# Four pairs of column blocks per feed-forward stage from seven products, with couples of products summed in PSUM

## The chip, the cores and the metric

The kernel runs on one core of one Trainium2 chip. Its engines work beside one another and meet at semaphores: TensorE (PE, with its weight loads as PEld), VectorE (DVE), ScalarE (ACT), GpSimd (POOL) and SyncE (SP, here a queue of transfers). The metric is device time in microseconds, the median of several runs. A profile shows one execution.

## The reference

Two transformer blocks over one sequence of 256 positions with a model width of 1024, in fp32. Between them lie four feed-forward stages of one form, two in the first block and two in the second; the rest (convolution, attention, gated delta rule, shared keys and values) is not touched by the change.

```python
def swiglu_ffn(h, w13, w2):
    gate, up = jnp.split(h @ w13, 2, axis=-1)
    return (jax.nn.silu(gate) * up) @ w2
...
x = x + 0.5 * swiglu_ffn(rms_norm(x, ffn1_norm[l]), ffn1_w13[l], ffn1_w2[l])
```

`w13` is 1024 x 5632 (2816 gate columns, 2816 up columns) and `w2` is 2816 x 1024.

## The kernel before

**Precision.** A product of fp32 matrices is made of three matmuls (`mm3`): each operand is split into a high part and the rest, and high x high, rest x high and high x rest are summed in PSUM. A weight unit is 128 x 1024; ScalarE copies it into the high part `wh` (L442, every activation of the kernel is recorded at this line) and VectorE subtracts to get the rest `wl` (L445, likewise every two-operand operation of VectorE). There are seven `wh` and seven `wl` buffers, and a buffer comes free with the last matmul on it. Matmuls stand at L468 (at L746 in the changed kernel where they belong to a pair), transposes at L471.

**Blocks.** The hidden width is cut into eleven blocks *j* of 256 gate and 256 up columns, the sequence into two row tiles T of 128. A plain block takes 2 T x 8 k-tiles x 3 = 48 matmuls with 512 columns each (`single`, `singles`). `act` makes the hidden activations from a block's PSUM tile (a Silu on ScalarE, a scale-and-multiply on VectorE), `flip` transposes them (two PE transposes, a copy on ScalarE, a subtract on VectorE), and `outs(j)` multiplies them by `w2` (24 matmuls into the four `acc` tiles).

**Pairs.** Two blocks *j*, *j2* together are a 2 x 2 block product (row tiles by halves of the 1024 inputs by blocks), which the kernel makes of seven products in place of eight (`pair`), each of 12 matmuls: 84 in place of 96. The products take sums of the activations (`forms`, once per stage) and running sums of the weights, kept in the tiles `n["11"]`, `n["12"]`, `n["21"]`, `n["22"]` (two 128 x 1024 units each, pool `s4`). `raw` loads such a tile with transfers of SP's queue; `more` adds a second weight onto it by accumulating transfers that GpSimd issues (L726); `plus` adds on VectorE. Within p2 the tile "11" gets its second weight by `more`, so the sequence is: VectorE ends the split of "11" for p1, the accumulating transfer runs, and then the split for the next product on "11", p5, can start. Before, the order of products was p1, p2, p7, p5, p6, p3, p4, each in a PSUM tile of its own, and VectorE (ScalarE for p1 and p5) added each into the SBUF tiles `t[0]` to `t[3]`.

**Order.** Instructions of an engine run in the order in which a scheduler wrote them down; `merged` deals the steps of pairs among steps of `singles` and `outs` evenly, and `ahead` names a priority in a table of numbers that the change leaves as it is. The stages are f1, a mixer, f2 (about 323 to 500 us), the delta rule, f3, a small stage, the shared keys and values, f4, and the end. In each of f1 to f4 three pairs are made of products, (2,3), (5,6), (8,9), and the blocks 0, 1, 4, 7, 10 are plain.

Of the kernel before, what the change touches and what calls it, by code (L numbers as in the profile page):

```python
# [12 lines left out]
AF = mybir.ActivationFunctionType  # L13
ALU = mybir.AluOpType
# [7 lines left out]
NB = 11  # L22
# [339 lines left out]
class _Kernel:  # L362
# [254 lines left out]
    def ffn(self, gain, w13, w2, alpha, first=False):  # L617
        D = self.D
# [9 lines left out]
        def run(leave):  # L628
            acc = self.accs()
# [31 lines left out]
            def out(j, T):  # L661
                while any(p[:2] == (j, T) for p in pend):
                    flip()
                if j not in wu:
                    wu[j] = [self.unit(D[w2][2 * j + i], None, 4 + i) for i in range(2)]
                self.proj_out(acc[T], hid[j], (0, 1), T, wu[j], j == 0, j == NB - 1)


            def singles(j):
# [23 lines left out]
            def forms():  # L693

                F = self.t("b8", (8, 256))
                S = self.hilo("b8", (8, 256))
                q = [[(slice(None), slice(4 * k, 4 * k + 4), self.tsl(T)) for k in range(2)] for T in range(2)]
                with self.ahead("f.sum." + self.stage):
                    for T in range(2):
                        c = (slice(None), slice(None), self.tsl(T))  # L700
                        self.tt(F[c], h[0][c].bitcast(F32), h[1][c].bitcast(F32), ALU.add)
                    (f11, f12), (f21, f22) = [[F[c] for c in r] for r in q]
                    self.tt(f22, f22, f21, ALU.subtract)
                    self.tt(f21, f11, f21, ALU.subtract)
                    self.tt(f11, f22, f11, ALU.add)
                    self.tt(f12, f11, f12, ALU.subtract)
                    for T, k in ((1, 1), (0, 0), (1, 0), (0, 1)):
                        c = q[T][k]
                        self.split(S[0][c], S[1][c], F[c])
                return S  # L710

            def pair(j, j2, S):

                n, t = {}, []

                def raw(name, jj, k0):
# [17 lines left out]
                def prod(a_, T, k0, w):  # L734
# [6 lines left out]
                    ps = self.t("mm")  # L741
                    for k in range(4):
                        c = slice((k % 2) * 512, (k % 2) * 512 + 512)
                        self.mm3(ps, a_, (slice(None), k0 + k, self.tsl(T)), u[k // 2], (slice(None), c),
                                 k == 0, k == 3)
                    return ps  # L746

                def add(o, a_, ps, op=ALU.add):
                    with self.ahead("f.ev." + self.stage):
                        self.tt(t[o], t[a_], ps, op)  # L750

                def neg(o, a_, ps):
                    with self.ahead("f.ev." + self.stage):
                        self.stt(t[o], t[a_], -1.0, ps, ALU.mult, ALU.subtract)

                def p1():
                    tmp = self.t("b8", (4, 512))
                    t.extend(tmp[:, i] for i in range(4))
                    raw("11", j, 0)
                    raw("12", j2, 0)  # L760
                    more("12", j2, 2)
                    ps = prod(h, 0, 0, "11")
                    with self.ahead("f.ev." + self.stage):
                        self.act(t[0], ps, AF.Copy)

                def p2():
                    raw("21", j, 2)
                    more("11", j2, 0)
                    add(3, 0, prod(h, 0, 4, "21"))
                    act(j, 0, t[3])  # L770

                def p7():
                    raw("22", j2, 2)
                    add(1, 0, prod(S, 1, 0, "12"))

                def p5():
                    ps = prod(S, 1, 4, "11")
                    with self.ahead("f.ev." + self.stage):
                        self.act(t[2], ps, AF.Copy)

                def p6():
                    plus("11", "22")
                    ps = prod(S, 0, 0, "11")
                    add(1, 1, ps, ALU.subtract)
                    add(0, 0, ps, ALU.subtract)
                    add(0, 0, t[2])
                    neg(2, 1, t[2])
                    act(j2, 1, t[2])

                def p3():  # L790
                    neg(0, 0, prod(S, 0, 4, "22"))
                    act(j2, 0, t[0])

                def p4():
                    plus("11", "21")
                    add(1, 1, prod(h, 1, 4, "11"))
                    act(j, 1, t[1])

                return [p1, p2, p7, p5, p6, p3, p4]

            def merged(few, many):

# [16 lines left out]
                        flip()  # L819

            single(0)
            single(1)
# [9 lines left out]
            out(10, 0)  # L832
            leave(0, self.resid(acc[0], x[0], alpha))
            out(9, 1)
            out(10, 1)
            leave(1, self.resid(acc[1], x[1], alpha))

        return enter, run
# [865 lines left out]
```

## Time and profile before

| | |
|---|---|
| median of three runs | 1236.3 us (1235.31 to 1239.24) |
| profiled execution | 1234.6 us, its span 1232.6 us |
| PE | 1198.6 us busy, 97% of the span |
| VectorE | 1004.5 us busy, 81% |
| ScalarE | 741.3 us busy, 60% |
| GpSimd | 166.5 us busy, 14% |
| transfers | 234.38 MB, 190 GB/s in the mean |

Busy times are shares of the whole span. Spans of neighbouring matmuls overlap in the records, and so do neighbouring instructions of VectorE by some 0.08 us, so that the pace of a row of instructions is read from their starts.

### The profile page before, as it was taken

To read this page: it belongs to the slowest core of one execution; us is meant where nothing else is said; L and a number is where in the kernel's file an instruction comes from. 1 tells how busy PE (TensorE), PEld (TensorE's weight loads), DVE (VectorE), ACT (ScalarE), POOL (GpSimd) and SP (SyncE) were. 2 spreads that over 40 slices of the span, in tenths; PEclk is the share of its full clock that TensorE was granted. 3 is DMA by queue.
4 is the path that set the end of the run, shared out by engine and by line. 5 is a ranking of instruction groups with operands and counts; after the bars stand their busy time and mean duration, and the time that the engine had idled before them with its cause. 6 is when DMAs were issued, how large, how long until landed. Compare 5 with 4: busy or idle time off the path is not lost.

```text
span 1232.6 us, 17134 instructions
## 1 busy us (share of the span) xinstructions
PE 1198.6 (97%) x6248; PEld 1002.1 (81%) x6248; DVE 1004.5 (81%) x1482; ACT 741.3 (60%) x1134; POOL 166.5 (14%) x223
## 2 busy tenths in 40 slices
PE   8999999998999999998899999999999999999998
PEld 6788888986888888898898888888777788888887
DVE  6799987998788998689755888998776859889964
ACT  6566666346666665875313765666675747566653
POOL 1110002001101000226703101000121201010000
PEclk9999999999999999999999999999999999999999
DMA  8989463414679836355412689936445349698262
GB/s 284 303 275 295 115 208 127 159 38 154 222 239 292 283 91 217 127 203 162 137 52 69 242 252 285 279 102 210 161 151 175 111 144 302 257 295 217 92 199 80
DMA packets 72853, 234.38 MB, mean 190 GB/s; under 512 B 13496, under 2 KB 16224, under 8 KB 72640
## 3 DMA queue, kind: packets, MB, share of 16 engines
q1 hardware_dynamic: 61008, 204.14, 47.9%
q0 software_dynamic: 7168, 25.85, 11.0%
q10 hardware_dynamic: 4592, 3.29, 0.9%
q8 instruction: 49, 0.80, 0.3%
q14 instruction: 36, 0.29, 0.1%
HBM read 230.86 MB, written 2.37 MB: 189 GB/s over the span
## 4 chain that ended last, share of the span: by engine, by line
PE 79%; DVE 8%; DMA 4%; ACT 4%; issue 2%; POOL 1%; SPq 0%; DVEq 0%; ACTq 0%; POOLq 0%
PE mm L468 48%; PE acc L468 28%; DVE wl L445 3%; PE mm L471 3%; DMA wr<-w 2%; ACT s L442 1%; ACT wh L442 1%; DVE b L452 1%; DVE s L452 1%; DMA wr<-g_qkv 1%; POOL t L445 1%; DMA wr<-g_gate 1%; ACT b L442 1%; DMA s<-w 1%; ACT L442 1%
## 5 line engine op out<-in xcount | busy, mean ns | idle before, releaser
L468 PE MATMUL mm<-wh,b 128*128 128x512 f32 (+3 forms) x1808 | 571.5, 390 | 2.6 <-ACT wh L442 0.9
L445 DVE TENSOR_TENSOR wl<-wr,wh 128x1024 fp32r<-128x1024 f32 (+2 forms) x290 | 355.2, 1235 | 67.9 <-ACT wh L442 65.5
L442 ACT ACTIVATE wh<-wr 128x1024 fp32r<-128x1024 f32 (+2 forms) x290 | 303.8, 1056 | 157.6 <-PE mm L468 50.6
L468 PEld LDWEIGHTS mm<-wh,b 128*128 128x128 f32 x1808 | 333.4, 188 | 75.9 <-ACT b L442 1.9
L468 PE MATMUL mm<-wl,b 128*128 128x512 f32 (+3 forms) x904 | 349.2, 387 | 3.5 <-DVE wl L445 3.5
L468 PE MATMUL acc<-wh,s 128*128 128x512 f32 x768 | 254.9, 399 | 3.2 <-DVE s L452 3.1
L442 ACT ACTIVATE wh<-s 128x1024 fp32r<-128x1024 f32 x168 | 177.4, 1061 | 96.6 <-PE acc L468 33.0
L445 DVE TENSOR_TENSOR wl<-s,wh 128x1024 fp32r<-128x1024 f32 x168 | 202.8, 1220 | 30.2 <-ACT wh L442 29.7
L468 PEld LDWEIGHTS mm<-wl,b 128*128 128x128 f32 x904 | 170.0, 188 | 37.9 <-DVE wl L445 4.8
L468 PEld LDWEIGHTS acc<-wh,s 128*128 128x128 f32 x768 | 144.8, 189 | 36.9 <-ACT s L442 4.5
L468 PE MATMUL acc<-wl,s 128*128 128x512 f32 x384 | 153.4, 399 | 0.0
L468 PE MATMUL mm<-b,wh 128*128 128x256 f32 x640 | 118.3, 285 | 1.3 <-DVE b L452 1.3
L468 PEld LDWEIGHTS mm<-b,wh 128*128 128x128 f32 x640 | 98.7, 189 | 2.3 <-DVE b L452 1.5
L726 POOL DMA_DIRECT2D s<-w x48 | 41.9, 893 | 403.2 <-DMA s<-w 255.2
L468 PE MATMUL mm<-b,wl 128*128 128x256 f32 x320 | 89.3, 285 | 0.0
L468 PEld LDWEIGHTS acc<-wl,s 128*128 128x128 f32 x384 | 72.9, 190 | 16.2
L448 POOL TENSOR_SCALAR t<-t 128x1 f32<-128x1 f32 (+3 forms) x41 | 20.5, 499 | 462.5 <-ACT s L442 392.6
L452 DVE SCALAR_TENSOR_TENSOR b<-mm,cols,b 128x128 fp32r<-128x128 f32 (+4 forms) x164 | 62.3, 410 | 23.2 <-ACT b L442 22.7
L471 PE MATMUL mm<-const,s 128*128 128x128 f32 x336 | 66.4, 278 | 6.5 <-DVE s L445 3.0
L471 PEld LDWEIGHTS mm<-const,s 128*128 128x128 f32 x336 | 43.6, 142 | 21.3 <-DVE s L445 5.2
L468 PEld LDWEIGHTS mm<-b,wl 128*128 128x128 f32 x320 | 59.8, 189 | 0.2 <-DVE wl L445 0.2
L445 DVE TENSOR_TENSOR s<-s,s 128x1024 f32<-128x1024 f32 x48 | 57.7, 1218 | 0.3
(164 smaller groups left out, 1183.6 us busy)
## 6 DMA issues: line engine op xcount, KB each, us to landing
wr<-w SPq DMA_DIRECT2D x168, 512.0 KB, 4.9
s<-w SPq DMA_DIRECT2D x96, 512.0 KB, 6.9
s<-w POOLq DMA_DIRECT2D x48, 512.0 KB, 9.5
wr<-g_qkv SPq DMA_DIRECT2D x24, 512.0 KB, 4.3
wr<-pg SPq DMA_DIRECT2D x16, 512.0 KB, 4.2
wr<-w_kv SPq DMA_DIRECT2D x16, 512.0 KB, 4.0
wr<-w_ag SPq DMA_DIRECT2D x8, 512.0 KB, 4.3
wr<-w_qk SPq DMA_DIRECT2D x8, 512.0 KB, 4.7
```

Of the source, the lines that this page charges most:

```text
L442: return self.nc.scalar.activation(out=out, in_=in_, func=func, **kw)
L445: return (eng or self.nc.vector).tensor_tensor(out=out, in0=in0, in1=in1, op=op)
L448: return (eng or self.nc.vector).tensor_scalar(out=out, in0=in0, scalar1=s1, scalar2=s2, op0=op0, op1=op1)
L452: return self.nc.vector.scalar_tensor_tensor(out=out, in0=in0, scalar=scalar, in1=in1, op0=op0, op1=op1)
L468: return self.nc.tensor.matmul(out, lhsT=lhsT, rhs=rhs, start=start, stop=stop)
L471: return self.nc.tensor.transpose(out=out, in_=in_, identity=self.con("ident"))
L726: self.tc.keep_in_program_order(self.nc.gpsimd.dma_start(out=n[a_][i], in_=D[w13][jj][k0 + i], accum_op=ALU.add))
```

## The change

Each feed-forward stage makes four pairs of products, (2,3), (4,5), (6,7), (8,9), called the first to the fourth pair here, and keeps the blocks 0, 1 and 10 plain. The order within a pair is p1, p2, p5, p3, p6, p7, p4. Three couples share a PSUM tile: p2 is accumulated onto p1 (tile "A" of the code), p3 onto p5 ("D"), p7 onto p6 ("E"). Between the two products of a couple the first one's value is read out: ScalarE copies A into `t[0]` and D into `t[2]`, and VectorE subtracts `t[1]` from E. The accumulating transfers stay (two units onto "12", two onto "11" per pair), two `plus` add on VectorE as before, and with a fourth pair there are more of both. In f1 (`first`) the plain block 10 is dealt among the first pair's products; in the other stages block 1 is. The end of a stage has the outputs of blocks 8 and 9.

```diff
+                    ps = self.t("mm") if on is None else on
...
+                                stop=k == 3 and i == 2, skip_group_check=on is not None)
...
+                    n["A"] = prod(h, 0, 0, "11")
+                    ev(self.act, t[0], n["A"], AF.Copy)
 
                 def p2():
                     raw("21", j, 2)
                     more("11", j2, 0)
-                    add(3, 0, prod(h, 0, 4, "21"))
-                    act(j, 0, t[3])
+                    act(j, 0, prod(h, 0, 4, "21", n["A"]))
+
+                def p5():
+                    raw("22", j2, 2)
+                    n["D"] = prod(S, 1, 4, "11")
+                    ev(self.act, t[2], n["D"], AF.Copy)
+
+                def p3():
+                    plus("11", "22")
+                    ev(self.tt, t[1], t[0], prod(S, 0, 4, "22", n["D"]), ALU.add)
+
+                def p6():
+                    n["E"] = prod(S, 0, 0, "11")
+                    ev(self.tt, t[1], n["E"], t[1], ALU.subtract)
+                    act(j2, 0, t[1])
...
-                    raw("22", j2, 2)
-                    add(1, 0, prod(S, 1, 0, "12"))
...
-                    add(1, 1, ps, ALU.subtract)
-                    add(0, 0, ps, ALU.subtract)
-                    add(0, 0, t[2])
-                    neg(2, 1, t[2])
+                    plus("11", "21")
+                    ev(self.tt, t[0], t[0], prod(S, 1, 0, "12", n["E"]), ALU.subtract)
+                    ev(minus, 2, 0, t[2])
                     act(j2, 1, t[2])
...
-                return [p1, p2, p7, p5, p6, p3, p4]
+                return [p1, p2, p5, p3, p6, p7, p4]
...
-            few = pair(2, 3, S)
-            merged(few[:2], singles(4) + outs(0))
-            merged(few[2:], outs(1) + outs(4) + singles(7))
-            merged(pair(5, 6, S), outs(2) + outs(3) + outs(7))
-            merged(pair(8, 9, S), outs(5) + outs(6))
-            merged([], singles(10))
-            merged([], outs(8))
+            few, pB, pC, pD = (pair(j, j + 1, S) for j in (2, 4, 6, 8))
+            merged(few[:2], singles(10 if first else 1) + outs(0))
+            if first:
+                merged(few[2:] + pB + pC + pD, outs(1) + outs(10) + sum((outs(i) for i in range(2, 8)), []))
+            else:
+                merged(few[2:], outs(1) + singles(10))
+                merged(pB + pC + pD, outs(2) + outs(3) + outs(10) + sum((outs(i) for i in range(4, 8)), []))
```

The first place is ScalarE in f2, where the value of p1 is copied out. Before, in the last pair (8,9), the copy of p1's tile `mm_873` stands ahead of the two splits of "11" for p5 (`wh_898` and `wh_900`, from the tiles `s4_865` and `s4_866` which the accumulating transfers write):

```order
L442 ACTIVATE s2_861_4201<-mm_863_4203 128x2x128
L442 ACTIVATE wh_896_4329<-wr_895_4327 128x1024
L442 ACTIVATE b8_864_4208<-mm_873_4227 128x512
L442 ACTIVATE wh_898_4345<-s4_865_4209 128x1024
L442 ACTIVATE s2_861_4201<-mm_874_4241 128x2x128
L442 ACTIVATE s2_828_4055<-mm_875_4246 128x2x128
L442 ACTIVATE wh_900_4349<-s4_866_4210 128x1024
```

After the change, in the last pair of f2, also (8,9), the same copy (`b8_903` from `mm_912`) stands behind both splits of "11" for p5 (`wh_928`, `wh_930`):

```order
L442 ACTIVATE wh_924_4439<-wr_923_4437 128x1024
L442 ACTIVATE s1_885_4291<-b8_831_4058,t_638_3250 128x256
L442 ACTIVATE wh_928_4459<-s4_904_4365 128x1024
L442 ACTIVATE s1_895_4335<-b8_831_4058,t_638_3250 128x256
L442 ACTIVATE wh_930_4463<-s4_905_4366 128x1024
L442 ACTIVATE s2_900_4357<-mm_902_4359 128x2x128
L442 ACTIVATE wh_937_4490<-wr_936_4488 128x1024
L442 ACTIVATE b8_903_4364<-mm_912_4383 128x512
```

The copy moved from ahead of the two splits that need the transfer to behind them, and the next row shows that PE now needs it.

The second place is PE at the same point, from the last use of p1's second unit (`wl_911`) to the start of p2. Before, p2 starts a new tile, `mm_885`:

```order
L468 MATMUL mm_873_4227<-wl_872_4224,b8_600_3064 128x512
L468 MATMUL mm_873_4227<-wh_871_4223,b8_601_3065 128x512
...
L471 MATMUL mm_875_4246<-const_98,s1_860_4198 128x128 x2
L468 MATMUL mm_885_4283<-wh_881_4275,b8_600_3064 128x512
```

After the change p2 goes on in p1's tile, `mm_912`, with two matmuls of an output and two transposes between:

```order
L746 MATMUL mm_912_4383<-wh_910_4379,b8_604_3074 128x512
L746 MATMUL mm_912_4383<-wl_911_4380,b8_604_3074 128x512
L746 MATMUL mm_912_4383<-wh_910_4379,b8_605_3075 128x512
L471 MATMUL mm_913_4397<-const_98,s1_886_4292 128x128 x2
L468 MATMUL acc_609_3129<-wh_924_4439,s2_871_4234 128x512
L468 MATMUL acc_609_3129<-wl_925_4440,s2_871_4234 128x512
L746 MATMUL mm_912_4383<-wh_916_4408,b8_604_3074 128x512
L746 MATMUL mm_912_4383<-wl_917_4409,b8_604_3074 128x512
```

So the first matmul of p2 now follows the copy on ScalarE.

The third place is VectorE in f2's third pair, (6,7), where p6 is read between p6 and p7. The list ends with that read (`b8_831` from `mm_878`):

```order
L445 TENSOR_TENSOR wl_889_4298<-wr_887_4295,wh_888_4297 128x1024
L445 TENSOR_TENSOR wl_891_4314<-s4_832_4059,wh_890_4313 128x1024
L445 TENSOR_TENSOR wl_893_4318<-s4_833_4060,wh_892_4317 128x1024
L445 TENSOR_TENSOR wl_899_4342<-wr_897_4339,wh_898_4341 128x1024
L445 TENSOR_TENSOR s2_872_4235<-mm_873_4236,s2_871_4234 128x2x128
L445 TENSOR_TENSOR b8_831_4058<-mm_878_4249,b8_831_4058 128x512
```

On PE nine matmuls of an output lie between the end of p6 and p7's first matmul on the same tile:

```order
L746 MATMUL mm_878_4249<-wh_876_4245,b8_646_3266 128x512
L468 MATMUL acc_609_3129<-wh_888_4297,s2_828_4051 128x512
L468 MATMUL acc_609_3129<-wl_889_4298,s2_828_4051 128x512
L468 MATMUL acc_609_3129<-wh_888_4297,s2_829_4052 128x512
...
L746 MATMUL mm_878_4249<-wh_881_4269,b8_645_3265 128x512
L746 MATMUL mm_878_4249<-wl_882_4270,b8_645_3265 128x512
```

Before, p6 had a tile of its own, and no matmul of p7 followed on its read.

## Rows read from the trace of the kernel before

**Rows 1.** The page: share of each engine, and PE's granted clock in 40 slices.
```profile
PE 1198.6 (97%) x6248; PEld 1002.1 (81%) x6248; DVE 1004.5 (81%) x1482; ACT 741.3 (60%) x1134; POOL 166.5 (14%) x223
...
PEclk9999999999999999999999999999999999999999
```

**Rows 2.** Stretches f1 and f2: length, busy PE, PEld, DVE, ACT, POOL, clock, transfers.
```profile
0.00:195.00 195.00, 189.54 (x833) 151.33 (x834) 162.19 (x202) 125.08 (x177) 17.07 (x31) 1.00 0.76 239
...
320.00:500.00 180.00, 179.96 (x806) 145.44 (x805) 156.17 (x192) 115.81 (x160) 13.71 (x17) 1.00 0.73 228
```

**Rows 3.** The chain that ended last, a piece in f2: start, us, what.
```profile
383.94 13.83 PE mm L468 x60
```

**Rows 4.** Groups of instructions in f2 by form: busy us, mean ns, idle before.
```profile
L445 DVE TENSOR_TENSOR wl<-s,wh 128x1024 fp32r<-128x1024 f32 x42 | 50.7, 1220 | 6.7 <-ACT wh L442 6.6
...
L442 ACT ACTIVATE wh<-s 128x1024 fp32r<-128x1024 f32 x42 | 44.5, 1061 | 23.1 <-PE acc L468 10.2 <-PE mm L468 6.7 <-DVE s L445 2.8
...
L445 DVE TENSOR_TENSOR s<-mm,s 128x256 fp32r<-128x256 f32 x22 | 8.6, 415 | 0.0
...
L452 DVE SCALAR_TENSOR_TENSOR s<-b,t,s 128x256 f32<-128x256 f32 x12 | 5.7, 478 | 0.0
```

**Rows 5.** Timeline of VectorE in f2: start, us, what.
```profile
418.67 0.69 DVE L445 TENSOR_TENSOR b<-b,mm 128x512 f32<-128x512 f32 x1
419.28 2.35 DVE L445 TENSOR_TENSOR wl<-s,wh 128x1024 fp32r<-128x1024 f32 x2
421.55 2.35 DVE L445 TENSOR_TENSOR s<-s,s 128x1024 f32<-128x1024 f32 x2
...
434.66 1.22 DVE L445 TENSOR_TENSOR wl<-s,wh 128x1024 fp32r<-128x1024 f32 x1
...
441.13 0.69 DVE L445 TENSOR_TENSOR b<-b,mm 128x512 f32<-128x512 f32 x1 [0.42 <-PE mm L468]
```

**Rows 6.** Timeline of GpSimd in f2's third pair: the second accumulating transfer's issue.
```profile
436.17 0.86 POOL L726 DMA_DIRECT2D s<-w  x1 [0.87 <-DVE wl L445]
```

**Rows 7.** Issue to landing (last figure), onto "11", second pairs of f1 to f4.
```profile
s<-w POOLq DMA_DIRECT2D x1, 512.0 KB, 10.5
...
s<-w POOLq DMA_DIRECT2D x1, 512.0 KB, 9.4
...
s<-w POOLq DMA_DIRECT2D x1, 512.0 KB, 10.0
...
s<-w POOLq DMA_DIRECT2D x1, 512.0 KB, 8.2
```

**Rows 8.** The same for the third pairs of f1 to f4.
```profile
s<-w POOLq DMA_DIRECT2D x1, 512.0 KB, 6.8
...
s<-w POOLq DMA_DIRECT2D x1, 512.0 KB, 6.6
...
s<-w POOLq DMA_DIRECT2D x1, 512.0 KB, 6.4
...
s<-w POOLq DMA_DIRECT2D x1, 512.0 KB, 8.1
```

**Rows 9.** All accumulating transfers of the kernel, issue to landing.
```profile
DMA to landing us min/median/max: 5.2/9.5/16.0
```

**Rows 10.** Timeline of ScalarE in f2's third pair.
```profile
444.13 0.60 ACT L442 ACTIVATE b<-mm 128x512 f32<-128x512 f32 x1 [0.28 <-PE mm L468]
...
448.14 1.06 ACT L442 ACTIVATE wh<-s 128x1024 fp32r<-128x1024 f32 x1 [1.79 <-PE acc L468]
```

**Rows 11.** Timeline of PE in f2's third pair.
```profile
440.69 0.40 PE L468 MATMUL mm<-wh,b 128*128 128x512 f32 x1
...
442.77 0.40 PE L468 MATMUL mm<-wl,b 128*128 128x512 f32 x1
```

**Rows 12.** Stretches within f2's second and third pair, columns as in rows 2.
```profile
390.00:400.00 10.00, 10.00 (x46) 8.08 (x45) 8.36 (x11) 6.50 (x9) 1.72 (x2) 1.00 1.04 303
...
430.00:440.00 10.00, 10.00 (x45) 8.08 (x44) 10.00 (x13) 6.43 (x8) 1.72 (x2) 1.00 0.58 135
```

More of the change, by code (lines that the diff above doesn't have):

```diff
@@ L665, in out @@
                     wu[j] = [self.unit(D[w2][2 * j + i], None, 4 + i) for i in range(2)]
-                self.proj_out(acc[T], hid[j], (0, 1), T, wu[j], j == 0, j == NB - 1)
+                self.proj_out(acc[T], hid[j], (0, 1), T, wu[j], j == 0, j == 9)
             def singles(j):
@@ L703, in forms @@
                     self.tt(f22, f22, f21, ALU.subtract)
-                    self.tt(f21, f11, f21, ALU.subtract)
+                    self.tt(f21, f21, f11, ALU.subtract)
                     self.tt(f11, f22, f11, ALU.add)
@@ L732, in plus, with prod @@
                             self.tt(n[a_][i], n[a_][i], n[b_][i], ALU.add)
-                def prod(a_, T, k0, w):
+                def prod(a_, T, k0, w, on=None):
                     u = []
@@ L740, in prod, with ev, minus @@
                         u.append(hl)
-                    ps = self.t("mm")
+                    ps = self.t("mm") if on is None else on
                     for k in range(4):
                         c = slice((k % 2) * 512, (k % 2) * 512 + 512)
-                        self.mm3(ps, a_, (slice(None), k0 + k, self.tsl(T)), u[k // 2], (slice(None), c),
-                                 k == 0, k == 3)
+                        lh, rh = (slice(None), k0 + k, self.tsl(T)), (slice(None), c)
+                        for i, (p, q) in enumerate(((0, 0), (0, 1), (1, 0))):
+                            self.nc.tensor.matmul(
+                                ps, lhsT=a_[p][lh], rhs=u[k // 2][q][rh], start=on is None and k == i == 0,
+                                stop=k == 3 and i == 2, skip_group_check=on is not None)
                     return ps
-                def add(o, a_, ps, op=ALU.add):
+                def ev(f, *args):
                     with self.ahead("f.ev." + self.stage):
[L750 to L754, printed above, removed]
+                        f(*args)
+                def minus(o, a_, ps):
+                    self.stt(t[o], t[a_], -1.0, ps, ALU.mult, ALU.subtract)
                 def p1():
@@ L761, in p1 @@
                     more("12", j2, 2)
-                    ps = prod(h, 0, 0, "11")
-                    with self.ahead("f.ev." + self.stage):
-                        self.act(t[0], ps, AF.Copy)
+                    n["A"] = prod(h, 0, 0, "11")
+                    ev(self.act, t[0], n["A"], AF.Copy)
                 def p2():
@@ L768, in p2 @@
                     more("11", j2, 0)
-                    add(3, 0, prod(h, 0, 4, "21"))
-                    act(j, 0, t[3])
-                def p7():
-                    raw("22", j2, 2)
-                    add(1, 0, prod(S, 1, 0, "12"))
[L776 to L783, printed above, removed]
-                    add(1, 1, ps, ALU.subtract)
-                    add(0, 0, ps, ALU.subtract)
-                    add(0, 0, t[2])
-                    neg(2, 1, t[2])
+                    act(j, 0, prod(h, 0, 4, "21", n["A"]))
[10 more added lines that the diff above has]
+                    act(j2, 0, t[1])
+                def p7():
+                    plus("11", "21")
+                    ev(self.tt, t[0], t[0], prod(S, 1, 0, "12", n["E"]), ALU.subtract)
+                    ev(minus, 2, 0, t[2])
                     act(j2, 1, t[2])
-                def p3():
-                    neg(0, 0, prod(S, 0, 4, "22"))
-                    act(j2, 0, t[0])
                 def p4():
-                    plus("11", "21")
-                    add(1, 1, prod(h, 1, 4, "11"))
-                    act(j, 1, t[1])
-                return [p1, p2, p7, p5, p6, p3, p4]
+                    ev(self.tt, t[3], t[0], prod(h, 1, 4, "11"), ALU.add)
+                    act(j, 1, t[3])
+                return [p1, p2, p5, p3, p6, p7, p4]
             def merged(few, many):
@@ L821, in run @@
             single(0)
-            single(1)
+            if first:
+                single(1)
             S = forms()
-            few = pair(2, 3, S)
-            merged(few[:2], singles(4) + outs(0))
-            merged(few[2:], outs(1) + outs(4) + singles(7))
-            merged(pair(5, 6, S), outs(2) + outs(3) + outs(7))
-            merged(pair(8, 9, S), outs(5) + outs(6))
-            merged([], singles(10))
-            merged([], outs(8))
+            few, pB, pC, pD = (pair(j, j + 1, S) for j in (2, 4, 6, 8))
+            merged(few[:2], singles(10 if first else 1) + outs(0))
+            if first:
+                merged(few[2:] + pB + pC + pD, outs(1) + outs(10) + sum((outs(i) for i in range(2, 8)), []))
+            else:
+                merged(few[2:], outs(1) + singles(10))
+                merged(pB + pC + pD, outs(2) + outs(3) + outs(10) + sum((outs(i) for i in range(4, 8)), []))
+            while pend:
+                flip()
+            out(8, 0)
             out(9, 0)
-            out(10, 0)
             leave(0, self.resid(acc[0], x[0], alpha))
+            out(8, 1)
             out(9, 1)
-            out(10, 1)
             leave(1, self.resid(acc[1], x[1], alpha))
```

## The prediction

> **What bounds the kernel now.** I first read the page's busy shares: PE is busy for 97% of the span, VectorE for 81%, and PE's granted clock is full in all 40 slices [rows 1]. So at first sight fewer matmuls mean less time. Then the stretches: in f2 PE is busy 179.96 of 180 us while VectorE has 156.17 and ScalarE 115.81; f1 has some loss in its first 70 us, which the change leaves in the same order [rows 2]. The chain that ended last says the same: in f2 it runs from matmul to matmul, 60 of them in 13.83 us, which is 0.2305 us for one [rows 3]; between neighbours the pace is 0.23. So PE sets the time of the four stages. But VectorE has only 24 us to spare in f2, and the fourth pair needs more of it, so the groups on VectorE and ScalarE [rows 4] and the transfers between them [rows 7, 8] decide how much of PE's gain is kept.
>
> **The gain.** A pair of blocks takes 84 matmuls in place of 96, so each stage loses 12, the kernel 48. 48 x 0.2300 = 11.0 us [rows 3]. Nothing else on PE changes: the outputs and transposes are the same in number.
>
> **VectorE's and ScalarE's work.** By the order's counts a stage gains six splits, four weight sums and has four evictions fewer on VectorE. From start to start a split or a sum takes 1.14 us ((421.55 - 419.28) / 2) and an eviction of 128 x 512 takes 0.61 (419.28 - 418.67) [rows 5]: 10 x 1.14 - 4 x 0.61 = 9.0 us a stage. Then f2 has 156.2 + 9.0 = 165.2 of 180.0 - 2.8 = 177.2 us, 93% [rows 2]. ScalarE gains six splits of 1.06 us [rows 4] and two copies of 0.60 [rows 10], 7.6 us, 123 of 177. Neither is over PE's time, so neither costs by its sum; their order and waits do.
>
> **The wait that the change makes.** Three steps of a pair hang on each other: VectorE ends p1's second split, the second accumulating transfer onto "11" is issued, and when it has landed ScalarE and VectorE split the sum for p5. In f2's third pair the split starts at 434.66 and lasts 1.22 [rows 5], the issue starts 0.3 us after its end [rows 6], the transfer takes 6.6 us [rows 8], and ScalarE takes it up at 448.14 [rows 10], 12.0 us after the issue, 5.4 after the landing. Before, PE makes p2 and p7 ahead of p5, and the transfer is hidden. Now p7 comes late, PE has 8.6 to 11.7 us from p1 to p5 by its order, and VectorE has only 7.0 to 9.4 us of other work between the two splits. Call L the time from issue to landing, and lead the time by which p1's second split ends ahead of its first matmul.
>
> Behind p5's split two things are queued that PE now waits for.
>
> *The copy of A.* In the fourth pair of f2, f3 and f4 ScalarE's order has the copy behind both splits of "11", a transposed activation and an output's split, and PE's p2 follows the copy. From p1's second split to the end of the copy: 0.3 + L + 1.06 (split) + 0.38 (activation) + 1.06 (split) + 0.60 (copy) + 0.05; PE gets from that split's first matmul to p2 in 1.8 us (seven matmuls, two transposes). PE waits L + 1.6 - lead. In f1 this order stands in the third pair instead, at the same price. In the other pairs it gives L - 1.1 or L - 0.5, below the lead.
>
> *The read of E.* p7 follows VectorE's read of p6. From the landing VectorE must do ScalarE's split first (1.06) and then, by its order in the third pair, 17 splits or sums x 1.14, three transposed activations at 0.33, a gate multiply at 0.40 (415 and 478 ns less the 0.08 by which neighbours overlap [rows 4, 5]) and two reads at 0.60: 22.0 us. PE has 23.0 us of matmuls over that way. PE waits L + 0.3 + 1.06 + 0.1 + 22.0 - 23.0 - lead = L + 0.5 - lead (L + 0.7 in f4). In the second and fourth pairs it is L - 0.9 at most, below the lead. That a read starts 0.04 us after its last matmul ends (440.69 + 0.40 to 441.13) is in these sums [rows 5, 11].
>
> *Lead.* A split waits for a buffer out of seven. By the order the seventh split before is used up on PE 45 matmuls (10.3 us) ahead of this one's first use in the third pair and 42 (9.6 us) in the fourth; less ScalarE's 1.06 and VectorE's 1.22 this leaves at most 8.0 and 7.3 us. The trace before shows 6.9 in f2's third pair (435.88 to 442.77) [rows 5, 11]. I take the caps, since PE's waits in a pair let the other engines come up again; 7.0 is the low bound.
>
> *L.* No row shows it under the new order. The eight nearest are the second transfers onto "11" in the second pairs, 8.2 to 10.5 [rows 7], and in the third pairs, 6.4 to 8.1 [rows 8]; the difference goes with the other transfers, whose share is 1.04 in the one and 0.58 in the other [rows 12]. Over all accumulating transfers it is 5.2 to 16.0 with a median of 9.5 [rows 9]. The new third pair has a pair behind it, as the second had before, and the fourth has none; I take the mean of the eight, 8.25, for both.
>
> The Trainium skill says otherwise, in "DMA: Bandwidth & Descriptors", section "Anatomy of one DMA — SWDGE (gpsimd) path": a transfer issued from GpSimd takes about 2.0 us plus its bytes over 436e3 a microsecond; for these 524,288 bytes that makes 3.2 us, an estimate. The trace disagrees with it here: no accumulating transfer lands within 5.2 us [rows 9]. By the page no wait would arise, and the sum would be 1225; by the rows it is the next paragraph's.
>
> **The sum.** Third pair, 8.25 + 0.5 - 8.0 = 0.7; fourth pair, 8.25 + 1.6 - 7.3 = 2.5; so 3.2 us each in f2, f3 and f4 (0.2 more in f4). f1: 8.25 + 1.6 - 8.0 = 1.8. Together 9.6 + 0.2 + 1.8 = 11.6 us lost, 11.0 won. Against the profiled execution, 1234.6 + 0.6 = 1235.2, and its median stands 1.7 us above it, so 1236.9; I write **1236**. Splitting L by place (9.5 for third pairs, 7.0 for fourth) comes to 2.0 and 1.3 a stage and 3.1 in f1, 13.2 in all, 1.6 us more: not far. Transfers as such cost nothing: f2's share of 0.73 [rows 2] grows by the sum of a fourth pair's and stays below 1 over the stage. The end of a stage costs nothing: between p4's last matmul and the transposes of its activations stand 14 matmuls, 3.2 us, over an eviction, a Silu and a multiply of 1.5.
>
> **Rivals.**
> *Faster, part of the wait hidden.* The transfers land as in the third pairs before, 7.0 us: fourth pair 1.3 x 3, third pair nothing, f1 0.6, together 4.5 lost. 1236.3 - 11.0 + 4.5 = 1230. For it: in the fourth pair no load of a further pair runs beside it. Against: the third does have one.
> *Faster, all hidden.* Below L = 5.7 nothing is left to wait for: 1225. Rows 9's lowest is 5.2, but none of the eight is below 6.4. The page's rule would give this.
> *Slower, by loaded transfers.* L is 9.5 in every pair and the lead 7.0: third pair 3.0, fourth 4.1, times three, f1 4.1, f4 0.2 more: 25.6 lost, 1236.3 + 14.6 = 1251. It decides from about L - lead = 2.3, where the losses pass the gain by 3.7. For it: pairs follow each other without the plain blocks between, so a share near 1.04 lasts [rows 12].
> *Slower, VectorE is late.* A pair takes VectorE up to 33.6 us by its order and PE 33.9. If VectorE stands still at each landing for the 0.2 to 2.6 us that its other work (7.0 to 9.4) doesn't cover of 0.3 + 8.25 + 1.06, mean 1.4, a pair lasts 35.0 and three pairs of four stages lose 3 x 4 x 1.1 = 13.2 us, in place of the reads' 2.3, while the copies' 9.3 stay: 22.5 lost, 1248. Against: seven buffers let it work ahead in the stretches of outputs.
>
> **How the numbers follow.** Chances: the forecast 0.38 (its own range 1231 to 1242, from L 7.4 to 9.0), part hidden 0.22, all hidden 0.12, loaded transfers 0.15, VectorE late 0.13. A measurement tells 0.3%, 3.7 us, from no change. Faster (below 1232.6): 0.34 and a small part of the forecast's, 0.36; slower (above 1240.0): 0.28 and a part of the forecast's, 0.32; same 0.32. The range from 1226 to 1247 leaves out the case of all hidden for the most part and the far end of the slower ones.
>
> **What would show it.** PE has 48 matmuls fewer and its pace stays 0.23. In f2, PE's idle time names ScalarE's copy once in the fourth pair (2.5 us, ahead of an accumulating matmul of p2) and VectorE's read of E in the third (0.7); ScalarE's idle time ahead of p5's split names the transfer, with L near 8. f2 lasts about as long as before. I am wrong if L is far from 8, if the lead is far from 7 to 8, if waits stand in first and second pairs too (VectorE late), or if PE has no waits at all.

## The result, and the profile after

The changed kernel takes 1255.8 us (median; 1252.8 to 1255.9) against 1236.5 (four runs of each): the ratio is 1.0142, with a 95% interval from 1.0119 to 1.0165. So it is slower by 19 us by the medians and by 18 us by the ratio, where no change had been forecast. The profiled execution took 1255.86 us, its span is 1254.1.

The page's first lines answer to [rows 1]: PE has 48 matmuls fewer and yet is busy 2.9 us longer, and the granted clock falls below 90% in some slices (a 9 stands for 90% or more).

```profile
span 1254.1 us, 17149 instructions
...
PE 1201.5 (96%) x6200; PEld 996.5 (79%) x6200; DVE 1036.8 (83%) x1506; ACT 765.1 (61%) x1166; POOL 178.3 (14%) x239
...
PEclk9999889999899999999989999999999999999999
```

By stretches (f1, then f2; length, busy PE, PEld, DVE, ACT, POOL, clock, transfers), against [rows 2]:

```profile
0.00:211.00 211.00, 193.25 (x821) 153.10 (x822) 170.99 (x207) 131.90 (x185) 20.48 (x35) 0.96 0.76 231
...
337.00:518.00 181.00, 179.42 (x797) 143.19 (x796) 165.01 (x199) 122.04 (x168) 17.35 (x22) 1.00 0.78 239
```

f1 is 16 us longer at a mean clock of 0.96; f2 is as long as before. VectorE's 165.01 us in f2 and ScalarE's 122.04 stand against the forecast 165.2 and 123.

A ruler for all runs is the start of the last output matmul of each stage on PE's timeline. From one to the next, in us, in the profiled executions (the column "to end of mixer" has what lies between f1 and f2, "to end of f3" also the delta rule, "to end of f4" also the shared keys and values):

| kernel | to end of f1 | to end of mixer | to end of f2 | to end of f3 | to end of f4 | span |
|---|---|---|---|---|---|---|
| before | 195.2 | 124.8 | 180.9 | 371.8 | 326.4 | 1232.6 |
| changed | 211.2 | 125.7 | 180.9 | 373.3 | 329.5 | 1254.1 |
| f1_as_others | 201.1 | 127.0 | 180.3 | 375.8 | 330.4 | 1248.1 |
| no_a | 207.0 | 129.1 | 182.1 | 375.8 | 330.7 | 1258.2 |
| half_sum | 204.4 | 128.4 | 179.2 | 374.0 | 326.5 | 1246.1 |
| own_sum | 212.1 | 125.7 | 181.9 | 376.5 | 335.0 | 1264.8 |
| pin | 201.1 | 133.7 | 179.2 | 380.9 | 328.6 | 1257.2 |
| pin_one | 197.5 | 129.0 | 179.1 | 380.2 | 328.0 | 1247.4 |
| pin_mix | 199.1 | 130.8 | 178.9 | 380.0 | 328.1 | 1250.5 |
| no_e | 206.0 | 129.1 | 182.4 | 376.3 | 330.7 | 1258.1 |
| f1_old | 195.0 | 127.1 | 180.8 | 373.9 | 329.7 | 1240.0 |
| only_f1 | 208.4 | 128.1 | 181.0 | 374.5 | 327.5 | 1253.1 |
| f1_old_half | 194.6 | 123.4 | 180.3 | 377.2 | 326.6 | 1235.3 |
| f1_old_p34 | 194.6 | 125.0 | 180.7 | 375.1 | 326.8 | 1236.3 |

A stretch with the same order of instructions differs from run to run by 1 to 4 us (the mixer takes 124.8, 127.1, 125.0 and 123.4 us in the four rows that have its old order), so a single column tells only differences of 3 us or more, and the medians tell the rest.

Of the changed kernel's 21.5 us, 16.0 arise in f1, though it has 2.8 us of matmuls fewer: it loses 18.8. Where PE waits in f1, by the view of waits (what waits, for what: sum, times, longest):

```profile
PE mm L471 <- DVE s L452: 4.4, 3, 2.4
PE acc L468 <- ACT s L442: 4.0, 1, 4.0
PE mm L746 <- ACT b L442: 2.6, 1, 2.6
...
PE mm L746 <- DVE b L445: 1.3, 1, 1.3
```

The third row is the copy of A, the fourth VectorE's read of E; the first two are a gate multiply ahead of its transposes and a transposed activation ahead of an output, two places that the prediction did not price. What they come from is on ScalarE's timeline at f1's third pair (start, us, what, idle before):

```profile
118.46 0.49 ACT L442 ACTIVATE s<-b,t 128x256 f32<-128x256 f32 x1
125.20 1.06 ACT L442 ACTIVATE wh<-s 128x1024 fp32r<-128x1024 f32 x1 [6.24 <-DMA s<-w]
126.16 0.49 ACT L442 ACTIVATE s<-b,t 128x256 f32<-128x256 f32 x1
128.16 1.06 ACT L442 ACTIVATE wh<-s 128x1024 fp32r<-128x1024 f32 x1 [1.51 <-DMA s<-w]
129.12 0.37 ACT L442 ACTIVATE s<-mm 128x256 fp32r<-128x256 f32 x1
129.39 1.05 ACT L442 ACTIVATE wh<-wr 128x1024 fp32r<-128x1024 f32 x1
130.34 0.59 ACT L442 ACTIVATE b<-mm 128x512 f32<-128x512 f32 x1
```

ScalarE stands still for 6.24 us and again for 1.51 ahead of p5's two splits, until the two accumulating transfers have landed; behind them come the Silu (126.16), the transposed activation (129.12), and the copy of A (130.34). PE's timeline at the same place:

```profile
127.23 0.69 PE L471 MATMUL mm<-const,s 128*128 128x128 f32 x2 [2.43 <-DVE s L452]
127.57 0.78 PE L468 MATMUL acc<-wh,s 128*128 128x512 f32 x1
130.98 0.79 PE L746 MATMUL mm<-wh,b 128*128 128x512 f32 x1 [2.63 <-ACT b L442]
131.57 0.63 PE L746 MATMUL mm<-wl,b 128*128 128x512 f32 x1
131.99 1.05 PE L746 MATMUL mm<-wh,b 128*128 128x512 f32 x2
```

PE does one output matmul between two waits, and after them a matmul starts every 0.42 us (131.57 to 131.99) in place of 0.23. The granted clock says why (stretches of f1, columns as above):

```profile
124.00:131.00 7.00, 1.93 (x9) 1.06 (x7) 4.23 (x5) 4.29 (x7) 0.85 (x1) 0.71 0.77 140
131.00:134.00 3.00, 3.00 (x8) 2.37 (x9) 2.85 (x5) 1.43 (x4) 0.00 (x0) 0.53 0.65 213
134.00:140.00 6.00, 6.00 (x27) 4.88 (x26) 4.33 (x6) 4.20 (x5) 0.00 (x0) 1.00 0.35 94
```

In 131 to 134 us the clock is 0.53 of full while PE is never idle: nearly all of it at the lower level, 1.2 of 2.4 GHz; from 134 on it is full again. The same happens behind the 4.0 us wait at 165 to 170 us:

```profile
170.00:175.00 5.00, 5.00 (x13) 3.90 (x13) 5.00 (x7) 1.17 (x2) 0.00 (x0) 0.52 0.32 105
```

Why the transfers land so late is seen on SP's queue just ahead of them, and in the issues and queues (issue and time to landing; then share of each kind, in 118 to 122 and in 122 to 126 us):

```profile
114.04 0.33 SPq L492 DMA_DIRECT2D wr<-w  x1
114.46 1.33 SPq L721 DMA_DIRECT2D s<-w  x3
```

```profile
s<-w POOLq DMA_DIRECT2D x1, 512.0 KB, 10.9
...
q1 hardware_dynamic: 261, 0.95, 68.3%
q0 software_dynamic: 54, 0.22, 29.2%
...
q0 software_dynamic: 187, 0.70, 90.2%
```

SP's queue had waited 4.0 us for one buffer, until a split on VectorE ended at 113.98, and then issued four loads in a row at 114.0 to 115.4 us; the accumulating transfers (q0) were issued right behind, at 115.6 and 117.1, had 29% of the engines' time in 118 to 122 us and 90% only after it, and landed after 9.4 and 10.9 us. In f2's third pair the issue (430.7 and 432.9) comes ahead of such loads (434.0 to 435.3), and the same transfers land in 5.3 and 7.4 us.

### The profile page after: what moved, and what is told of

Same layout as the page of the kernel before. It is cut to its first block, busy times and chain, and to the rows that moved or that the text cites. A ratio compares the mean times of both kernels' runs of the same rounds, so it can differ in the third digit from the quotient of the medians.

```text
span 1254.1 us, 17149 instructions
## 1 busy us (share of the span) xinstructions
PE 1201.5 (96%) x6200; PEld 996.5 (79%) x6200; DVE 1036.8 (83%) x1506; ACT 765.1 (61%) x1166; POOL 178.3 (14%) x239
## 4 chain that ended last, share of the span: by engine, by line
PE 58%; DVE 15%; DMA 4%; ACT 4%; issue 3%; POOL 2%; SPq 0%; DVEq 0%; ACTq 0%; POOLq 0%
PE mm L468 22%; PE acc L468 18%; PE mm L746 15%; DVE wl L445 7%; DVE s L445 2%; PE mm L471 2%; ACT wh L442 2%; ACT s L442 1%; DMA s<-w 1%; DVE s L452 1%; DMA wr<-g_gate 1%; DVE b L452 1%; POOL s L445 1%; POOL t L445 1%; DMA wr<-pp 1%
## 5 line engine op out<-in xcount | busy, mean ns | idle before, releaser
L442 ACT ACTIVATE wh<-wr 128x1024 fp32r<-128x1024 f32 (+2 forms) x258 | 270.2, 1057 | 127.3 <-PE acc L468 30.1
L445 DVE TENSOR_TENSOR wl<-wr,wh 128x1024 fp32r<-128x1024 f32 (+2 forms) x258 | 316.3, 1236 | 33.2 <-ACT wh L442 31.9
L442 ACT ACTIVATE wh<-s 128x1024 fp32r<-128x1024 f32 x224 | 236.3, 1059 | 147.0 <-DMA s<-w 45.4
L746 PE MATMUL mm<-wh,b 128*128 128x512 f32 x896 | 303.5, 401 | 7.6 <-DVE b L445 3.5
L445 DVE TENSOR_TENSOR wl<-s,wh 128x1024 fp32r<-128x1024 f32 x224 | 269.4, 1217 | 34.8 <-ACT wh L442 34.3
L468 PE MATMUL mm<-wh,b 128*128 128x512 f32 (+3 forms) x880 | 269.3, 382 | 3.8 <-DVE b L452 1.9
L468 PE MATMUL acc<-wh,s 128*128 128x512 f32 x768 | 262.6, 404 | 8.6 <-ACT s L442 4.0
L746 PE MATMUL mm<-wl,b 128*128 128x512 f32 x448 | 177.9, 397 | 0.8 <-DVE wl L445 0.8
L468 PE MATMUL mm<-wl,b 128*128 128x512 f32 (+3 forms) x440 | 166.2, 379 | 2.7 <-DVE wl L445 2.7
L726 POOL DMA_DIRECT2D s<-w x64 | 56.0, 936 | 470.5 <-DMA s<-w 221.3
L471 PE MATMUL mm<-const,s 128*128 128x128 f32 x336 | 67.4, 279 | 11.8 <-DVE s L452 6.3
```

The source lines that it names most:

```text
L442: return self.nc.scalar.activation(out=out, in_=in_, func=func, **kw)
L445: return (eng or self.nc.vector).tensor_tensor(out=out, in0=in0, in1=in1, op=op)
L468: return self.nc.tensor.matmul(out, lhsT=lhsT, rhs=rhs, start=start, stop=stop)
L471: return self.nc.tensor.transpose(out=out, in_=in_, identity=self.con("ident"))
L726: self.tc.keep_in_program_order(self.nc.gpsimd.dma_start(out=n[a_][i], in_=D[w13][jj][k0 + i], accum_op=ALU.add))
L746: self.nc.tensor.matmul(ps, lhsT=a_[p][lh], rhs=u[k // 2][q][rh], start=on is None and k == i == 0, stop=k == 3 and i == 2, skip_group_che ...
```

## The experiments

The runs were made in three groups, each beside the kernel before (medians 1236.9, 1235.9 and 1237.2 us). Theory *chain*, called *queue* in the second group: what is lost comes from the wait for the accumulating transfer onto "11", passed on by the order on ScalarE. Its rivals are f1's own dealing of the steps, the shared PSUM tiles as such, and VectorE.

**f1_as_others.** f1 takes the dealing of f2 to f4.

```diff
-            if first:
-                single(1)
...
-            merged(few[:2], singles(10 if first else 1) + outs(0))
-            if first:
+            merged(few[:2], singles(1) + outs(0))
+            if False:
```

> Stage f1 deals its steps as the other three stages do (block 1 among the first pair's first products, block 10 among its others, then the outputs among the other three pairs); nothing else changes. Theory chain: f1 loses its time because the second accumulating transfer onto 11 lands 10.5 to 10.9 us after its issue and ScalarE's row of work stands behind it; then the dealing alone helps little, 1250 to 1256 us. Rival order: the loss is made by f1's own dealing, which leaves too little other work on ScalarE and VectorE between p1's splits and p5's; then f1 loses as f2 to f4 do, 4 to 6 us in place of 18.8, and the time is 1240 to 1244.

Measured: 1250.5 us, ratio 1.0104 (1.007 to 1.0138). The time lies at the low end of chain's range, but f1 is 10 us shorter (201.1): the dealing matters more than chain said, and less than order said. The first 70 us of f1 now have two waits of 2.8 us for VectorE (the work behind the second goes back to a load of 8.9 us); after them f1 keeps one wait, the read of E:

```profile
PE mm L746 <- DVE b L445: 1.3, 1, 1.3
```

The second transfer of the third pair takes 8.0 us in place of 10.9, and nothing that PE needs is late behind it.

**no_a.** p2 gets a tile of its own.

```diff
-                    act(j, 0, prod(h, 0, 4, "21", n["A"]))
+                    ev(self.tt, t[3], t[0], prod(h, 0, 4, "21"), ALU.add)
+                    act(j, 0, t[3])
```

> p2 gets a PSUM tile of its own again and VectorE adds it to t[0] (one 128x512 eviction more per pair); the other two couples stay. Theory chain: the copy is only one of the things that stand behind p5's split on ScalarE; its waits on PE (3.2 us in f1 and about 1.6 of slow clock after it, 0.2 to 0.6 in each other stage) go and those of the flips, the gate multiplies and the reads of E stay: 1249 to 1253 us. Rival couple: sharing the tile is what costs; then 10 us or more come back, below 1246.

Measured: 1262.9 us, ratio 1.0205 (1.0177 to 1.0234). Both are wrong: it is 7 us slower than the changed kernel. In the profiled execution, the fastest of its four, f1 gains 4.2 us and the other stretches lose 8.3, of which 3.4 in the mixer, where no pair stands. VectorE's added eviction is only 0.6 us a pair; f1 still ends 11.8 us later than before (207.0 against 195.2), so sharing tile A is not the main cost.

**no_e.** p7 gets a tile of its own.

```diff
                     ev(self.tt, t[1], n["E"], t[1], ALU.subtract)
+                    ev(self.tt, t[0], t[0], n["E"], ALU.subtract)
...
-                    ev(self.tt, t[0], t[0], prod(S, 1, 0, "12", n["E"]), ALU.subtract)
+                    ev(self.tt, t[0], t[0], prod(S, 1, 0, "12"), ALU.subtract)
```

> p7 gets a PSUM tile of its own (one 128x512 eviction more per pair on VectorE); the other two couples stay and nothing is pinned. Theory queue: the waits for VectorE's read of E go (1.45 us in f1, 0.7 in f2, 1.9 in f4), the queue behind p5's split stays: 1251 to 1254 us. Rival VectorE: it is the bound of the pairs, so work added to it makes the time longer: 1256 us or more.

Measured: 1260.0 us, ratio 1.0196 (1.0177 to 1.0215): slower again, as the rival has it. f2 takes 182.4 us against 180.9, where 0.7 less had been expected. That the 0.6 us more a pair on VectorE is the reason is not shown: the mixer has 3.4 us of the loss here too, with another order of its instructions (269 on VectorE in that stretch against 265), and the next run adds more to VectorE and is faster. No run gave p3 a tile of its own, so the couple D is not tested by itself.

**half_sum.** The second unit onto "11" is loaded by SP and added by VectorE.

```diff
-                    more("11", j2, 0)
+                    o = self.t("s4")
+                    with self.ahead("f.raw." + self.stage):
+                        self.tc.keep_in_program_order(self.nc.sync.dma_start(out=o, in_=D[w13][j2][1]))
+                    with self.ahead("f.cmb." + self.stage):
+                        self.tc.keep_in_program_order(self.nc.gpsimd.dma_start(
+                            out=n["11"][0], in_=D[w13][j2][0], accum_op=ALU.add))
+                        self.tt(n["11"][1], n["11"][1], o, ALU.add)
```

> Of the two units added onto 11, only the first is an accumulating transfer; the second is loaded by SP into a tile of its own and added by VectorE (1.14 us per pair more on VectorE). Theory chain, with the two transfers going one behind the other: alone, the transfer lands in 5.3 us, as where the two are issued 3 us apart, so f1's waits of 2.6, 3.2 and 4.2 us and the slow clock after them go, 12 to 15 us in all: 1241 to 1245 us. Rival VectorE: with 4.6 us more a stage VectorE is the bound of the pairs and the time stays at 1254 or rises.

Measured: 1251.0 us, ratio 1.0109 (1.008 to 1.0137): 5 us better, not 12 to 15. The single transfer of f1's third pair still took 9.3 us behind SP's loads, so its being one of two was only part of the delay; f2 (179.2) and f4 (326.5) are 1.7 and 3.0 us shorter; there PE waits for no read of E, and for a copy only once, 0.8 us in f4. VectorE is busier in this f2 than in the change's, 168.86 of 179 us against 165.01 of 181 (columns as above), so its load alone does not make a stage longer here:

```profile
333.00:512.00 179.00, 178.69 (x796) 143.26 (x796) 168.86 (x202) 121.41 (x165) 12.85 (x17) 1.00 0.76 241
```

**own_sum.** The sum gets tiles of its own, so that the transfer needn't wait for p1's splits.

```diff
                     raw("21", j, 2)
+                    raw("11", j, 0)
                     more("11", j2, 0)
```

> The sum for p5 gets tiles of its own: SP loads the first weight again, and the accumulating transfer no longer waits for p1's splits (two loads of 512 KB and two s4 tiles more per pair; the pool stays at 13). Theory chain: nothing behind p5's split waits any more; f1 loses 14 us less and the other stages up to 3 us each less: 1232 to 1241 us. Rival transfers: loads of the next pair come later because a pair now holds ten of thirteen tiles, and 32 loads more fill the queue: 1254 us or slower.

Measured: 1265.5 us, ratio 1.0229 (1.0201 to 1.0256): the rival's case. The accumulating transfers were issued no earlier:

```profile
117.46 0.85 POOL L726 DMA_DIRECT2D s<-w  x1 [8.25 <-DMA s<-w]
```

GpSimd waited for the load underneath, which came late; that a pair held ten of thirteen tiles is the rival's reason, argued and not shown apart. So this run did not take the wait away, and tells nothing on chain itself.

**pin.** An order on ScalarE alone: p5's two splits stand behind the copy of A.

```diff
-                            self.split(hl[0], hl[1], n[w][i])
+                            c = self.act(hl[0], n[w][i], AF.Copy)
+                            if after is not None:
+                                self.tc.add_manual_dep(c.ins, after.ins.name, mybir.DependencyInfo(
+                                    mybir.DependencyClass.NoSync, mybir.DependencyReason.DATA), reason="behind")
+                            self.tt(hl[1], n[w][i], hl[0].bitcast(F32), ALU.subtract)
...
-                    ev(self.act, t[0], n["A"], AF.Copy)
+                    n["cp"] = ev(self.act, t[0], n["A"], AF.Copy)
...
-                    n["D"] = prod(S, 1, 4, "11")
+                    n["D"] = prod(S, 1, 4, "11", after=n["cp"])
```

> p5's two splits on ScalarE are ordered behind the copy of A (an order on ScalarE only; no wait, no data and no arithmetic changes). Theory queue: PE waits not for the transferred sum itself, which p5 needs 8.6 us or more after p1, but for the copy, the transposed activations and the gate multiplies that stand behind the split that waits for it; with the splits behind the copy f1's waits of 2.6, 3.2 and 4.2 us and the slow clock after them go, some 14 us, and 1 to 2 us more in f2 to f4: 1238 to 1242 us. Rival transfer: the sum lands too late for PE itself; then p5 waits in place of p2 and the time stays above 1250.

Measured: 1255.6 us, ratio 1.0156 (1.0132 to 1.018): as slow as the change, and within the rival's number, not queue's; yet f1 is 10.1 us shorter, and the traces tell why. ScalarE at f1's third pair:

```profile
124.97 0.60 ACT L442 ACTIVATE b<-mm 128x512 f32<-128x512 f32 x1 [2.37 <-PE mm L750]
...
126.98 1.06 ACT L442 ACTIVATE wh<-s 128x1024 fp32r<-128x1024 f32 x1 [0.86 <-DMA s<-w]
130.41 1.06 ACT L442 ACTIVATE wh<-s 128x1024 fp32r<-128x1024 f32 x1 [2.37 <-DMA s<-w]
```

The transfers land as late as in the change (9.4 and 11.3 us), the copy goes ahead of them, and PE loses 0.3 us ahead of p2 where it had lost 5.8; the clock stays full there. Not all of it is won: later in the same pair PE now waits for the copy of D, which had no wait in the change:

```profile
139.34 0.50 PE L750 MATMUL mm<-wh,b 128*128 128x512 f32 x1 [2.02 <-ACT b L442]
```

In f1's fourth pair the two transfers were issued 3 us apart in this run and landed in 5.3 and 5.4 us, so the order's part there is not told apart from theirs. f2 is 1.7 us shorter, f4 0.9. What was won is lost behind f1 and f2: the mixer is 8 us longer, the way to f3's end 7.6. A part of that is seen on PE at the end of f1:

```profile
204.22 1.97 PE L471 MATMUL mm<-const,s 128*128 128x128 f32 x8 [2.75 <-ACT s L442]
```

The norm of the next stage's input stands behind splits of that stage's weights on ScalarE, which the scheduler has moved ahead there; the stretch 201 to 211 us has a clock of 0.66. So the rival "transfer" is out for p5, which starts without a wait (131.05), and a part of the gain is given back by an order elsewhere; the rest of the 8 us is not traced.

**pin_one** and **pin_mix.** The order of pin with f1 dealt as the other stages are (the diff of f1_as_others), and with f1's own start but its outputs dealt as in the others:

```diff
-                merged(few[2:] + pB + pC + pD, outs(1) + outs(10) + sum((outs(i) for i in range(2, 8)), []))
+                merged(few[2:], outs(1))
+                merged(pB + pC + pD, outs(2) + outs(3) + outs(10) + sum((outs(i) for i in range(4, 8)), []))
```

> The order of pin, and f1 deals its steps as the other stages do. Theory queue: f1 keeps the waits at its start that the run with that dealing showed (about 6 us, for loads), and the rest goes: 1240 to 1244 us, no faster than with f1's own dealing. Rival order: f1's own dealing is worse in itself; then this is the faster of the two.

> The order of pin, and f1 keeps its own start but deals the outputs of blocks 2 to 7 and 10 among the second to fourth pair alone, as the other stages do. Theory queue: within 2 us of pin, since the dealing matters only through what stands behind the split. Rival order: 3 us or more faster than pin.

Measured: 1249.3 us, ratio 1.0108 (1.0092 to 1.0123), and 1254.6 us, ratio 1.0146 (1.0115 to 1.0177). f1 takes 197.5 and 199.1 us: with both, pin_one's f1 loses 5.1 us (197.5 - 195.2 + 2.8) in place of 18.8, most of it at its start. Queue had pin_one no faster than pin, and it is 6 us faster, with an f1 3.6 us shorter, so the dealing is worth some 4 us by itself. pin_mix is 1.0 us faster than pin, as queue has it. Both keep the longer stretches behind f1 and f2.

**f1_old, only_f1, f1_old_half, f1_old_p34.** f1 is taken back whole, or f2 to f4 are; then f1_old with half_sum's or (in f3 and f4) pin's edit. The other stages keep their order on every engine. The change takes one difference of the activations with the opposite sign, and the old products in these four kernels leave out the matching change, so their values are not the reference's. Instructions, shapes and order are those of the two kernels, and only times are read from them.

```diff
-            single(0)
+            if first:
+                ...
+                merged(pair_old(5, 6, S), outs(2) + outs(3) + outs(7))
+                merged(pair_old(8, 9, S), outs(5) + outs(6))
+                ...
+            else:
+                ...
```

> Stage f1 is taken back whole (three pairs, each product in a tile of its own, its old order); f2, f3 and f4 have the change, and every engine's order in them is that of the changed kernel. Theory f1: f1 made 16.0 us of the loss (211.2 against 195.2 us at its end) and the stretch after it 0.9; the time is 1237 to 1241 us. Rival spread: the loss moves on to the next stage with loads that f1 delays or brings forward; 1245 us or more.

> The other half: f1 has the change, f2, f3 and f4 are taken back whole, with the order of the kernel before on every engine. Theory f1: 1250 to 1254 us (before and 16 to 17). Rival spread: below 1246.

> f1_old, and in f2 to f4 the second unit onto 11 is loaded apart and added by VectorE. Theory transfer: in f2 to f4 the read of E and the copy of A wait 2 to 5 us a stage because p5's split waits for the second accumulating transfer; the run with that sum on VectorE had f2 1.7 and f4 3.0 us shorter than the change, f3's stretch 0.7 longer; so 4 us faster than f1_old, 1233 to 1237 us. Rival VectorE: the added work brings back what the transfer gives, within 1 us of f1_old.

> f1_old, and in f3 and f4 p5's splits are ordered behind the copy of A on ScalarE (f2 stays, since pinned there the start of the next stage was 4 to 7 us later). Theory queue: f3 and f4 lose 1 to 1.5 us less each: 2 to 3 us faster than f1_old. Rival order elsewhere: the scheduler moves the weight splits of the stages that follow ahead of the norms and takes it back; no faster than f1_old, or slower.

Measured: f1_old 1241.8 us, ratio 1.0044 (1.0029 to 1.006); only_f1 1254.1, 1.0121 (1.0098 to 1.0144); f1_old_half 1239.5, 1.0022 (1.0012 to 1.0033); f1_old_p34 1240.4, 1.0031 (1.0014 to 1.0048). Against the kernel before in the same group the two halves of the change cost 4.6 us (f2 to f4) and 16.9 (f1). f1_old is just above its forecast (1237 to 1241), only_f1 at the upper end of its own (1250 to 1254). The other two gain 2.3 and 1.4 us on f1_old by the medians, less than the 4 and the 2 to 3 expected; f4 is 3.1 and 2.9 us shorter in both. None of the twelve is faster than the kernel before.

## Why the prediction was wrong

**Gain and work: right.** 48 matmuls fell away at 0.23 us, and VectorE's and ScalarE's sums in f2 are within 1.4 us.

**The mechanism: right at its root, with places missing.** Both waits that it names are there: the copy of A behind p5's splits, and the read of E. But of the 10.5 us that f1's last two pairs lose, only 3.2 are a wait for the copy; 3.1 are waits for gate multiplies and 4.2 a wait for a transposed activation, which hang on the same row of work on ScalarE and which the prediction did not price. In the four places that it priced, its formulas come within 0.5 us with the measured L and lead:

| place | L | lead | by the formula | measured wait of PE |
|---|---|---|---|---|
| f1 third pair, L + 1.6 - lead | 10.9 | 6.4 | 6.1 | 5.8 (2.65 + 3.2) |
| f1 fourth pair, L - 0.4 - lead | 10.5 | 6.6 | 3.5 | 4.7 (0.5 + 4.2) |
| f2 fourth pair, copy, L + 1.6 - lead | 5.3 | 6.9 | 0.0 | 0.2 |
| f2 third pair, read of E, L + 0.5 - lead | 7.4 | 7.6 | 0.3 | 0.7 |
| f4 third pair, read of E, L + 0.7 - lead | 9.3 | 7.6 | 2.4 | 1.9 |

(Waits are counted here as the time over the usual pace of 0.23 us, so they stand a little above the page's idle times.) The second row's formula is not in the prediction, which had that pair free of waits, and it misses by 1.2 us. The lead of f1's third pair can be read from p1's second split on VectorE, which starts at 115.63 and lasts 1.22 us, and from the first matmul on its result, at 123.27; the fourth pair's L from its two transfers, issued one right behind the other:

```profile
115.63 1.22 DVE L445 TENSOR_TENSOR wl<-s,wh 128x1024 fp32r<-128x1024 f32 x1
...
123.27 0.39 PE L746 MATMUL mm<-wl,b 128*128 128x512 f32 x1
...
154.75 1.74 POOL L726 DMA_DIRECT2D s<-w  x2 [10.86 <-ACT wh L442]
...
s<-w POOLq DMA_DIRECT2D x1, 512.0 KB, 10.5
```

pin shows for the third pair that this is the cause and not only a fit: it leaves the transfers as late as they were and reorders ScalarE, and the 5.8 us ahead of p2 are gone, though 2.0 come back ahead of p3.

**The failed step: L and lead in f1, "8.25 + 1.6 - 8.0 = 1.8".** I took one L for all pairs and the cap of the seven buffers for the lead. In f1's last two pairs L was 10.9 and 10.5 and the lead 6.4 and 6.6, below the 7.0 that the prediction called its low bound. By the traces the first L goes with the four loads that SP issued just ahead, the second with the transfer's own neighbour, issued 0.9 us before it; no run moved those loads alone, and why the lead was shorter is not traced. [Rows 7] had 10.5 for f1, and the text saw the two kinds of L in [rows 7, 8] and averaged them; f1's fourth pair it let go free. The two pairs cost 10.5 us in place of 1.8. How near the forecast stood to "slower" was also worked out wrongly: by its own terms, with one lead for all pairs, the losses are 7 (L - lead) + 8.1, so they pass the gain by 3.7 us at L - lead = 0.9, not at 2.3.

**A term that was missing: the granted clock.** After its two long waits (5.8 and 4.2 us) PE runs at the lower level: six matmuls behind the first, twelve behind the second, and eight more at 55 us, behind two waits of 0.9 and 0.8 us. Behind 22 of these the next one starts 0.43 us later in place of 0.23: 4.4 us. Before, the same two waits near 52 us (0.7 and 0.8) had no such matmuls behind them, so why the clock fell at 55 us stays open. The prediction read [rows 1] as a full clock in all 40 slices. In f2 and, behind its start, in f1 it was full, but not everywhere: before, the mixer's mean was 0.97, and there a wait of 3.1 us has matmuls at 0.43 us behind it (306.46 to 307.31 for two):

```profile
195.00:320.00 125.00, 117.09 (x792) 105.91 (x791) 109.78 (x266) 64.18 (x133) 14.79 (x19) 0.97 0.35 118
...
303.31 0.47 PE L468 MATMUL acc<-wh,s 128*128 128x512 f32 x1 [3.09 <-DVE s L452]
...
306.46 1.05 PE L468 MATMUL acc<-wh,s 128*128 128x512 f32 x2
307.31 0.63 PE L468 MATMUL acc<-wl,s 128*128 128x512 f32 x1
```

With the pairs' 10.5, the clock's 4.4, the read of E in the first pair (1.5, forecast at nothing) and 1.1 us more at the start, 17.5 of f1's 18.8 us are named; the rest I leave open.

**f2 to f4: near in sum, other in parts.** Forecast 3.2 us lost each. By the ruler f2 loses 2.8, f3's stretch 4.3, f4's 5.9, 13.0 in place of 9.8; less the 8.3 us of matmuls that fell away this is a net of 4.7, and f1_old's median is 4.6 over before. But the copy in the fourth pair costs 0.2, not 2.5, for L is 5.3 when the two transfers are issued 3 us apart and nothing else runs. In its place stand gate multiplies ahead of the last transposes (1.0 in f2; the prediction's "the end of a stage costs nothing" is wrong), and in f4 a slow start and the read of E. So that the sum comes near is in part luck. That VectorE is too near its limit, a rival at 0.13, is not borne out: no_a and no_e add 0.6 us a pair to it and lose 7 and 4, but half_sum adds more and has a shorter f2 and f4.

**The page's rule** of the Trainium skill ("DMA: Bandwidth & Descriptors", section "Anatomy of one DMA — SWDGE (gpsimd) path"), an estimate of 3.2 us, was not met: the fastest of 64 accumulating transfers took 5.2 us.

The rival "slower, by loaded transfers" (1251 us) is nearest to what happened, but the load is in f1's bursts, not in pairs that follow each other: f2 to f4 have these and land in 5.2 to 9.3 us.

## What to carry to other kernels

Where a shared PSUM tile puts an eviction on the path, look at what stands ahead of that eviction on its engine, and at the one wait there that is a transfer: that transfer's worst landing under a burst of loads, not its mean, is the price. Here the scheduler wrote the waiting instruction first; an order on that engine took most of the wait away, but re-dealt what follows, so judge such an edit stage by stage and not by the total. And where PE waits for some microseconds, look in the trace for matmuls at the lower clock behind the wait, and count them too.

## What the runs showed of the hardware

An accumulating transfer of 512 KB takes 5.2 to 5.3 us alone (f2, f3 and f4, fourth pairs), 7.4 to 10.5 in third and fourth pairs when another was issued 2.2 to 0.9 us before it, and 9.4 to 10.9 behind four loads of SP's queue. There the loads issued ahead of it went first: the transfer issued at 115.64 us moved its first packet at 120.30, 4.7 us later, against 1.6 us for the one issued at 465.47 in f2's fourth pair. In 117 to 118 us all packets of the two were SP's:

```profile
q1 hardware_dynamic: 109, 0.41, 106.6%
```
